# Adding the identity and r to G inside the PSUM bank: two products on TensorE for three additions on VectorE

## The chip, the cores and the metric

The kernel runs on one core of one Trainium2 chip. The metric is the device time of one execution in microseconds (us), the median of the runs of one kernel. The granted TensorE clock is given as a share of full speed: 1.00 is 2.4 GHz and 0.50 is 1.2 GHz.

## The reference, cut to what matters

The whole program is a small two-block network (512 tokens of 1024 channels, two expert layers, a gated MLP, an RWKV layer, two attention layers). The change touches only the recurrence of the RWKV layer:

```python
def _wkv_step(S, inp):
    r_t, w_t, k_t, v_t, a_t, b_t = inp
    sa = jnp.einsum('zbhvk,zbhk->zbhv', S, a_t)
    S = S * w_t[..., None, :] + sa[..., :, None] * b_t[..., None, :] + v_t[..., :, None] * k_t[..., None, :]
    return S, jnp.einsum('zbhvk,zbhk->zbhv', S, r_t)
...
def wkv_bidir(state0, scan_in):
    state, ys = lax.scan(_wkv_step, state0, scan_in)
```

It runs in both directions (z) over 256 context and 512 latent positions, for 16 heads of 64 channels.

## The kernel before, in words

The recurrence is not walked position by position. `rwkv_scan` cuts the 768 positions into 12 chunks of C = 64 (NCH = 12, four of the context and eight latent, `lat`) and the 16 heads into 8 pairs (KD = 8). A head pair is a **group** of 12 chunks; 8 x 12 = 96 chunks, called rounds here, follow one another.

Inside a group the chunks form a chain through the state SV. `Chain.period` issues one round: `py` of chunk g, `pg` of chunk g+1, `pa` of g+3, `ps` and `pz` of g+2 (the table `STAGES`). Each is one PSUM bank with a single buffer (pY, pG, pA, pS, pz), filled by TensorE (PE) and emptied by VectorE (DVE) and ScalarE (ACT):

- `pa` (L1534): the chunk's triangular scores, to SC2 by ACT (L1541) and, masked, by DVE (L1542).
- `ps` (L1544): the transposed k and b and their products with r, to SCB by ACT (L1554) and DVE (L1556).
- `pz` (L1559): SC2 times the solved triangular inverse XF, to Zx by ACT (L1566).
- `pg` (L1568): four products Zx x SCB into the bank pG. The upper 64 partitions of G are copied by ACT (L1583). The lower 64 get the identity added in the first 64 columns (L1575) and, for latent chunks, r times the decay (RH) in the last 64 (L1581, twice), all three on DVE.
- `py` (L1585): four products G x SV into pY. DVE scales the new state into SV (L1596), and the output Y is copied by ACT (L1606) or added by DVE (L1608).

The PE instructions of the chain keep their written order (class `Ordered`). All else is placed by the compiler's scheduler, which writes one fixed order for each engine: an instruction that waits holds up all that stand behind it on its engine.

Beside the chain, the next head pair is prepared: `scan_decay`, `scan_scaled` and `scan_r` compute decays and scaled keys, and `solve` inverts the triangular blocks. `solve` starts with a transposition into Mx on DVE (L1427). Then 62 small multiplications and additions on DVE (L1438 into sol, L1440 into Xx) and 48 on GpSimd (POOL; the same lines, sop) run beside one another; when both are done DVE transposes the result into XR and XL (L1444, L1445). PE takes XR in 24 products pv, ACT copies them to Vs (L1460) after copying parts of XL to XF (L1472), and PE runs 24 products px, which ACT copies to XF. No chunk of the next group can pass `pz` before that.

```python
STAGES = (("py", 0), ("pg", 1), ("pa", 3), ("ps", 2), ("pz", 2))
...
    for e, r0, r1, nm in ((nc.vector, 0, R.rows, "sol"), (nc.gpsimd, R.rows, 31, "sop")):
        for u in range(r0, 31):
```

Of the kernel before, what the change touches and what calls it, by code (L numbers as in the profile page):

```python
# [10 lines left out]
F32 = mybir.dt.float32  # L11
# [5 lines left out]
OP = mybir.AluOpType  # L17
# [3 lines left out]
P = 128  # L21
# [658 lines left out]
def moe(K, l, nt, rows, router, gain=None):  # L680
# [23 lines left out]
    with tc.tile_pool(name="mow", bufs=1) as wb, tc.tile_pool(name="mox", bufs=3) as s2, \  # L704
# [83 lines left out]
        for i, (r, u) in enumerate(units):  # L788
            pu = unit_mm(xT, weights("moe_wu", r), "pu")
            if i + 2 < n:  # L790
                gather(i + 2)
            hg = s2.tile([P, 256], F32, name="hg")
            nc.scalar.activation(hg, pg, AF.Silu)  # L793
            nc.vector.tensor_tensor(out=hg, in0=hg, in1=pu, op=OP.mult)  # L794
            if i + 1 < n:
                pg = unit_mm(xn, weights("moe_wg", units[i + 1][0]), "pg")
            elif gain is not None:
                nc.scalar.dma_start(T.gain, gain)
            hT = unit_hT(hg)
            xT, xn = xn, unit_in(i + 2) if i + 2 < n else None  # L800
            unit_out(i, hT, weights("moe_wd", r))
# [132 lines left out]
def expert_h(K, s2, pg, pu):  # L934
    nc = K.nc
    hg = s2.tile([P, 512], F32, name="hg")
    nc.scalar.activation(hg, pg, AF.Silu)
    nc.vector.tensor_tensor(out=hg, in0=hg, in1=pu, op=OP.mult)
    return hg
# [24 lines left out]
C = 64  # L964
# [215 lines left out]
def two(a, b):  # L1180

    return bass.AP(tensor=a.tensor, offset=a.offset, ap=[list(a.ap[0]), [b.offset - a.offset, 2], *[list(d) for d in a.ap[1:]]])
# [312 lines left out]
class Chain:  # L1495
# [72 lines left out]
    def pg(self, ch):  # L1568
        R, S, lat, nq = self.R, ch.S, ch.lat, ch.nq
        pg = R.p.tile([P, 2, 2, P], F32, name="pG")  # L1570
        for h in range(2):
            for z in range(2):
                self.pe.matmul(pg[:, h, z, :nq], lhsT=ch.Zx[:, h, z, :], rhs=ch.SCB[:, z, :2 if lat else 1, h, :], start=True, stop=True)
        ch.G = G = R.s3.tile([P, 2, 2, P], F32, name="G")
        d = [self.K.nc.vector.tensor_tensor(out=G[:C, :, :, :C].rearrange("p h z t -> p (h z) t"),  # L1575
                               in0=pg[:C, :, :, :C].rearrange("p h z t -> p (h z) t"),
                               in1=R.id2[:C, None, :].to_broadcast([C, 4, C]), op=OP.add)]
        if lat:
            for h in range(2):
                hs = slice(h * C, (h + 1) * C)  # L1580
                d.append(self.K.nc.vector.tensor_tensor(out=G[:C, h, :, C:], in0=pg[:C, h, :, C:],  # L1581
                                       in1=two(S.RH[hs, 0, ch.sl[0], h], S.RH[hs, 1, ch.sl[1], h]), op=OP.add))
        self.apart(self.K.nc.scalar.copy(G[C:, :, :, :nq], pg[C:, :, :, :nq]), d)  # L1583

    def py(self, ch):  # L1585
        R, S, nq, sl, vs, i = self.R, ch.S, ch.nq, ch.sl, ch.vs, ch.i
# [816 lines left out]
```

## Time and profile before

| what | value |
|---|---|
| median of 3 runs | 3281.62 us (3279.72 to 3285.73) |
| the profiled execution: its own time, its span | 3283.3 us, 3281.5 us |
| busy over the span: PE, DVE, ACT, POOL | 89%, 47%, 32%, 23% |
| mean granted TensorE clock | 0.930 |
| the scan's rounds, from the first to the last | about 1457 to 2095 us of the span |

Times of day are in us from the span's start. An engine is busy where one of its instructions runs; a line such as L1575 is a line of the code above. A product of float32 shows as two rows of the trace (two passes), so four products pG are eight passes. Rows of the windows view give the busy time of engines in a stretch, and behind each in brackets the number of instructions.

### The profile page before, as it was taken

The page shows a single profiled execution, that of the slowest core. Times are in us where ns is not written, and L with a number is a line of the kernel's source. Part 1 is how long each engine was busy: PE and PEld are TensorE (multiplying, and loading weights), DVE is VectorE, ACT ScalarE, POOL GpSimd, SP SyncE. Part 2 cuts the span into 40 slices and gives each one's busy share as a digit, 9 for nine tenths or more (in the row PEclk, how much of TensorE's full clock was granted, in tenths as well). Part 3 has the DMA queues.
Part 4 walks back from the last instruction along what each step waited for, and adds up shares of the span by engine and source line. Part 5 has one row for each costly group of instructions (what it writes and reads, how often), then busy time and mean ns, then how long its engine had stood idle before and what let it go on. Part 6 is the DMA issues. An engine that isn't in the chain of part 4 may idle for free. (4 is left out here: it accounts for less than half of the span.)

```text
span 3281.5 us, 51499 instructions
## 1 busy us (share of the span) xinstructions
PE 2909.2 (89%) x18992; PEld 2096.6 (64%) x18992; DVE 1547.4 (47%) x3550; ACT 1036.6 (32%) x2318; POOL 747.4 (23%) x949
## 2 busy tenths in 40 slices
PE   8999997999999799957777777889999987899998
PEld 4777786555554487647777776765555546777866
DVE  4342354100000498678777777541111126665584
ACT  4111231111111343355555555410000014544463
POOL 1022322111111100255556656221111110000000
PEclk9999997999999899968888878889999998999999
DMA  7555516899999624110111110569999994121200
GB/s 287 185 173 188 202 49 251 289 408 408 405 406 404 271 73 146 66 61 24 34 33 38 38 35 18 188 251 399 409 407 405 402 346 144 53 75 61 76 33 33
DMA packets 222836, 637.64 MB, mean 194 GB/s; under 512 B 37779, under 2 KB 65251, under 8 KB 222449
## 3 DMA queue, kind: packets, MB, share of 16 engines
q1 hardware_dynamic: 180048, 565.13, 45.3%
q10 hardware_dynamic: 27472, 45.72, 4.2%
q0 software_dynamic: 15056, 23.41, 2.0%
q8 instruction: 153, 2.51, 0.3%
q14 instruction: 107, 0.87, 0.1%
HBM read 609.24 MB, written 49.00 MB: 201 GB/s over the span
## 5 line engine op out<-in xcount | busy, mean ns | idle before, releaser
L793 ACT ACTIVATE hg<-pg 128x256 f32<-128x256 f32 x86 | 33.0, 383 | 790.4 <-PE pg L1489 790.4
L794 DVE TENSOR_TENSOR hg<-hg,pu 128x256 f32<-128x256 f32 x86 | 36.2, 421 | 522.5 <-PE pu L1489 515.3
L734 POOL DMA_INDIRECT xe<-hrow,idx x86 | 88.2, 1026 | 655.3 <-PE ptr L1489 619.2
L71 DVE TENSOR_TENSOR wl<-wr,wh 128x1024 fp32r<-128x1024 f32 (+1 forms) x140 | 168.9, 1221 | 117.8 <-ACT wh L70 117.1
L158 POOL TENSOR_TENSOR rs_r<-rs_t,nhalf 128x1 f32<-128x1 f32 (+2 forms) x52 | 58.2, 1121 | 728.2 <-DVE rs_t L156 387.6
L141 PE MATMUL ps<-hT,wh 128*128 128x512 f32 (+1 forms) x496 | 188.6, 381 | 6.2 <-DVE q L1951 3.0
L142 PE MATMUL ps<-hT,wh 128*128 128x512 f32 (+1 forms) x496 | 183.8, 371 | 0.0
L143 PE MATMUL ps<-hT,wl 128*128 128x512 f32 (+1 forms) x496 | 183.3, 370 | 0.0
L70 ACT CAST wh<-wr 128x1024 fp32r<-128x1024 f32 (+1 forms) x140 | 141.2, 1041 | 126.9 <-PE ps L143 45.4
L1489 PE MATMUL pu<-wx,xT 128*64 128x256 f32 x1520 | 176.8, 380 | 4.8 <-DMA wx<-in_moe_wu 4.8
L1489 PE MATMUL pd<-wx,hT 128*64 128x512 f32 x704 | 161.9, 598 | 18.4 <-issue 10.0
L1489 PE MATMUL pg<-wx,xT 128*64 128x256 f32 x1520 | 174.2, 379 | 1.1 <-DMA wx<-in_moe_wg 0.8
L764 DVE COPY hT<-pth 128x128 f32<-128x128 f32 x86 | 25.1, 292 | 313.6 <-ACT hT L763 313.6
L1489 PE MATMUL pd<-we,hT 128*64 128x512 f32 x672 | 155.1, 599 | 11.8 <-issue 6.5
L1489 PEld LDWEIGHTS pu<-wx,xT 128*64 128x64 f32 x1520 | 110.4, 137 | 84.3 <-issue 24.7
L1489 PE MATMUL pG<-SCB,Zx 128*128 128x128 f32 (+1 forms) x768 | 118.6, 303 | 39.3 <-DVE SCB L1556 19.0
L1489 PE MATMUL pu<-we,xT 128*64 128x256 f32 x1232 | 143.4, 380 | 6.8 <-DMA we<-in_moe_wu 6.7
L1489 PE MATMUL pg<-we,xT 128*64 128x256 f32 x1232 | 145.9, 387 | 2.8 <-DMA we<-in_moe_wg 1.2
L1489 PEld LDWEIGHTS pg<-wx,xT 128*64 128x64 f32 x1520 | 111.8, 137 | 54.7 <-issue 2.1
L779 POOL DMA_INDIRECT ybuf<-yo,idx x86 | 86.4, 1005 | 234.4 <-ACT yo L776 84.5
L1489 PEld LDWEIGHTS pG<-SCB,Zx 128*128 128x128 f32 x768 | 104.0, 210 | 47.8 <-ACT Zx L1566 29.0
L1489 PEld LDWEIGHTS pu<-we,xT 128*64 128x64 f32 x1232 | 88.6, 137 | 67.7 <-issue 15.6
(583 smaller groups left out, 6881.4 us busy)
## 6 DMA issues: line engine op xcount, KB each, us to landing
wx<-in_moe_wu SPq DMA_DIRECT2D x144, 512.0 KB
wx<-in_moe_wg SPq DMA_DIRECT2D x144, 512.0 KB
wx<-in_moe_wd SPq DMA_DIRECT2D x130, 512.0 KB
we<-in_moe_wd SPq DMA_DIRECT2D x126, 512.0 KB
we<-in_moe_wg SPq DMA_DIRECT2D x112, 512.0 KB
we<-in_moe_wu SPq DMA_DIRECT2D x112, 512.0 KB
w<-in_ada_w SPq DMA_DIRECT2D x96, 512.0 KB
wr<-in_ga_w_in SPq DMA_DIRECT2D x32, 512.0 KB
```

Source lines behind the costliest of these rows:

```text
L70: nc.scalar.copy(hi, x)
L71: nc.vector.tensor_tensor(out=lo, in0=x, in1=hi.bitcast(F32), op=OP.subtract)
L141: nc.tensor.matmul(ps, lhsT=a[0], rhs=b[0], start=start, stop=False, **kw)
L142: nc.tensor.matmul(ps, lhsT=a[0], rhs=b[1], start=False, stop=False, **kw)
L143: nc.tensor.matmul(ps, lhsT=a[1], rhs=b[0], start=False, stop=stop, **kw)
L158: nc.gpsimd.tensor_tensor(out=r, in0=t, in1=K.nhalf[:, :n], op=OP.pow)
L734: nc.gpsimd.indirect_dma_start(out=xe[i % 3], out_offset=None, in_=hhalf, in_offset=bass.IndirectOffsetOnAxis(ap=idx[:, u, 0, r:r + 1], ax ...
L764: nc.vector.tensor_copy(hT[:, 1], pt[:, 1])
L779: nc.gpsimd.indirect_dma_start(out=yhalf, out_offset=bass.IndirectOffsetOnAxis(ap=idx[:, u, 1, r:r + 1], axis=0), in_=yo, in_offset=None, ...
L793: nc.scalar.activation(hg, pg, AF.Silu)
L794: nc.vector.tensor_tensor(out=hg, in0=hg, in1=pu, op=OP.mult)
L1489: r = f(*a, **kw)
```

## The change

The four products of pG now open one accumulation over the whole bank. Two more products follow: id2 (two stacked 64 x 64 identities) times the identity matrix adds the identity to the first 64 columns of the lower half, in every round; id2 times RH adds r to the last 64 columns, in rounds of latent chunks. One ACT copy then takes all 128 partitions of G. The three additions on DVE are gone.

```diff
     def pg(self, ch):
         R, S, lat, nq = self.R, ch.S, ch.lat, ch.nq
         pg = R.p.tile([P, 2, 2, P], F32, name="pG")
+        f = dict(skip_group_check=True)
         for h in range(2):
             for z in range(2):
-                self.pe.matmul(pg[:, h, z, :nq], lhsT=ch.Zx[:, h, z, :], rhs=ch.SCB[:, z, :2 if lat else 1, h, :], start=True, stop=True)
-        ch.G = G = R.s3.tile([P, 2, 2, P], F32, name="G")
-        d = [self.K.nc.vector.tensor_tensor(out=G[:C, :, :, :C].rearrange("p h z t -> p (h z) t"),
-                               in0=pg[:C, :, :, :C].rearrange("p h z t -> p (h z) t"),
-                               in1=R.id2[:C, None, :].to_broadcast([C, 4, C]), op=OP.add)]
+                self.pe.matmul(pg[:, h, z, :nq], lhsT=ch.Zx[:, h, z, :], rhs=ch.SCB[:, z, :2 if lat else 1, h, :],
+                               start=(h == 0 and z == 0), stop=False, **f)
+
+        self.pe.matmul(pg[:C, :, :, :C], lhsT=R.id2, rhs=self.K.ident.rearrange("p (h t) -> p h t", h=2)[:, :, None, :].to_broadcast([P, 2, 2, C]),
+                       start=False, stop=True, **f)
         if lat:
-            for h in range(2):
-                hs = slice(h * C, (h + 1) * C)
-                d.append(self.K.nc.vector.tensor_tensor(out=G[:C, h, :, C:], in0=pg[:C, h, :, C:],
-                                       in1=two(S.RH[hs, 0, ch.sl[0], h], S.RH[hs, 1, ch.sl[1], h]), op=OP.add))
-        self.apart(self.K.nc.scalar.copy(G[C:, :, :, :nq], pg[C:, :, :, :nq]), d)
+            self.pe.matmul(pg[:C, :, :, C:].rearrange("p h z t -> p z h t"), lhsT=R.id2, rhs=two(S.RH[:, 0, ch.sl[0]], S.RH[:, 1, ch.sl[1]]),
+                           start=False, stop=True, **f)
+        ch.G = R.s3.tile([P, 2, 2, P], F32, name="G")
+        self.K.nc.scalar.copy(ch.G[:, :, :, :nq], pg[:, :, :, :nq])
```

The scheduler also writes another order. On PE, at the end of a solve in the middle of the scan, before (pY, pG, pA, pS are the chain's, pv and px the solve's):

```order
L1489 MATMUL pY<-SV,G 128x64 x4
L1489 MATMUL pG<-SCB,Zx_10725 128x128 x4
L1489 MATMUL pA<-BK_10717,AD_10719 128x128 x2
L1489 MATMUL pS<-ident,BK_10717 128x128 x2
L1458 MATMUL pv<-XR,MO 64x64 x24
L1458 MATMUL px<-XL,Vs 64x64 x24
```

And with the change:

```order
L1489 MATMUL pY<-SV,G 128x64 x4
L1458 MATMUL pv<-XR,MO 64x64 x24
L1489 MATMUL pG<-SCB,Zx_10725 128x128 x4
L1489 MATMUL pG<-ident,id_9924 64x4x64
L1489 MATMUL pG<-RI_10455,id_9924 64x2x2x64
L1489 MATMUL pA<-BK_10717,AD_10719 128x128 x2
L1489 MATMUL pS<-ident,BK_10717 128x128 x2
L1458 MATMUL px<-XL,Vs 64x64 x24
```

The products pv have moved ahead of the round's pG, pA and pS, and these now stand between pv and px.

On DVE, before, one round within the solve (SV to SV; sol and Xx are steps of the solve):

```order
L1596 TENSOR_TENSOR SV<-pY,WL 64x2x128
L1608 TENSOR_TENSOR Y<-pY,Y 64x128 x2
L1438 TENSOR_TENSOR sol<-Xx,Mx 128x98
L1575 TENSOR_TENSOR G<-pG,id_9924 64x4x64
L1581 TENSOR_TENSOR G<-pG,RI_10455 64x2x64 x2
L1440 TENSOR_TENSOR Xx<-Xx,sol 128x7x14
L1542 TENSOR_TENSOR SC_13360<-pA,mL 128x2x64
L1438 TENSOR_TENSOR sol<-Xx,Mx 128x91
L1440 TENSOR_TENSOR Xx<-Xx,sol 128x7x13
L1556 TENSOR_TENSOR SCB<-pS,mR 128x2x128
L1438 TENSOR_TENSOR sol<-Xx,Mx 128x84
L1440 TENSOR_TENSOR Xx<-Xx,sol 128x7x12
```

With the change, the end of the same solve:

```order
L1542 TENSOR_TENSOR SC_13292<-pA,mL 128x2x64
L1438 TENSOR_TENSOR sol<-Xx,Mx 128x21
L1440 TENSOR_TENSOR Xx<-Xx,sol 128x7x3
L1556 TENSOR_TENSOR SCB<-pS,mR 128x2x128
L1438 TENSOR_TENSOR sol<-Xx,Mx 128x14
L1440 TENSOR_TENSOR Xx<-Xx,sol 128x7x2
L1596 TENSOR_TENSOR SV<-pY,WL 64x2x128
L1438 TENSOR_TENSOR sol<-Xx,Mx 128x7
L1608 TENSOR_TENSOR Y<-pY,Y 64x128 x2
L1440 TENSOR_TENSOR Xx<-Xx,sol 128x7
L1444 STREAM_TRANSPOSE XR<-Xx 128x1024
L1445 STREAM_TRANSPOSE XL<-Xx 128x1024
```

Before, the rounds of the chain ran out at the step of 84 elements and 24 steps in a row followed; with the change the steps are spread over the rounds down to the last, and between Mx and XR stand no G, and two SC, one SCB, one SV and two Y (one row of x2) fewer.

## Rows read from the trace of the kernel before

**Rows 1.** Windows of all engines: the scan's rounds (busy PE, PEld, DVE, ACT, POOL; clock).

```profile
core 0: us, PE busy (x) PEld busy (x) DVE busy (x) ACT busy (x) POOL busy (x), PEclk, DMA share, GB/s
1457.50:2095.40 637.90, 493.44 (x4248) 459.31 (x4248) 498.25 (x1162) 344.40 (x877) 365.46 (x485) 0.82 0.11 33
```

**Rows 2.** Waits in the scan: who waited for whom, us in total, times, longest.

```profile
POOL Xx L1430 <- DVE XL L1445: 61.6, 6, 12.2
PE pv L1458 <- DVE XR L1444: 53.6, 7, 8.2
...
PE px L1458 <- ACT Vs L1460: 14.3, 7, 2.1
```

**Rows 3.** Windows of the seven solves, Mx to XR, all engines: their sum.

```profile
sum 258.00, PE 182.98 PEld 172.65 DVE 244.68 ACT 118.63 POOL 169.87; mean PE 26.14 PEld 24.66 DVE 34.95 ACT 16.95 POOL 24.27
```

**Rows 4.** The same seven windows, tile sol alone (DVE's solve): shortest, longest, sum.

```profile
1741.20:1776.90 35.70, 20.08 (x62) 0.98 0.08 23
...
1996.90:2035.90 39.00, 23.45 (x62) 0.98 0.08 21
sum 258.00, DVE 148.53; mean DVE 21.22
```

**Rows 5.** The same seven windows, tile G alone: their sum.

```profile
sum 258.00, PE 52.08 PEld 48.24 DVE 44.98 ACT 29.04; mean PE 7.44 PEld 6.89 DVE 6.43 ACT 4.15
```

**Rows 6.** The same seven windows, tile sop alone (POOL's part of the solve): their sum.

```profile
sum 258.00, POOL 151.46; mean POOL 21.64
```

**Rows 7.** Timeline at the end of one solve (start, us, instruction).

```profile
1684.51 0.25 POOL L1440 TENSOR_TENSOR Xx<-Xx,sop 128x24 f32<-128x24 f32 x1
...
1691.43 1.25 DVE L1444 STREAM_TRANSPOSE XR<-Xx 128x1024 f32<-128x1024 f32 x1
1692.60 1.86 DVE L1445 STREAM_TRANSPOSE XL<-Xx 128x1024 f32<-128x1024 f32 x1
...
1692.73 4.45 PE L1458 MATMUL pv<-XR,MO 32*64 32x64 f32 x48 [7.45 <-DVE XR L1444]
1694.49 3.41 ACT L1472 COPY XF<-XL 32x384 f32<-32x384 f32 x4 [8.65 <-DVE XL L1445]
...
1697.91 2.58 ACT L1460 COPY Vs<-pv 32x192 f32<-32x192 f32 x8
...
1699.23 4.44 PE L1458 MATMUL px<-XL,Vs 32*64 32x64 f32 x48 [2.06 <-ACT Vs L1460]
```

**Rows 8.** Groups by line in the scan: the G instructions, and a copy of 128 partitions.

```profile
L1575 DVE TENSOR_TENSOR G<-pG,id 64x256 f32<-64x256 f32 x95 | 39.1, 411 | 9.9 <-PE pG L1489 8.9
L1583 ACT COPY G<-pG 64x512 f32<-64x512 f32 x64 | 37.2, 581 | 88.7 <-issue 65.7 <-PE pG L1489 13.7 <-ACT Y L1606 4.2
L1581 DVE TENSOR_TENSOR G<-pG,RI 64x128 f32<-64x128 f32 x128 | 35.5, 278 | 1.9
L1554 ACT COPY SCB<-pS 128x256 f32<-128x256 f32 x95 | 35.4, 373 | 19.9 <-PE pS L1489 17.2 <-DVE km L1406 2.3 <-PE pz L1489 0.3
...
L1583 ACT COPY G<-pG 64x256 f32<-64x256 f32 x31 | 11.4, 367 | 31.0 <-PE pG L1489 18.1 <-DVE SC L1542 4.0 <-DMA kT<-kD 3.3
```

**Rows 9.** Groups of the page, expert layers: products with 64 columns of weights, 256 moving.

```profile
L1489 PE MATMUL pu<-wx,xT 128*64 128x256 f32 x1520 | 176.8, 380 | 4.8 <-DMA wx<-in_moe_wu 4.8
```

**Rows 10.** Windows of two pA (four passes each): busy PE, clock.

```profile
1717.60:1718.90 1.30, 1.17 (x4) 0.50 0.00 0
1723.00:1723.70 0.70, 0.66 (x4) 1.00 0.70 225
```

**Rows 11.** Windows, all engines: four rounds of the last group; then 17 us behind a solve.

```profile
2071.10:2084.40 13.30, 13.30 (x122) 13.30 (x121) 8.12 (x24) 9.87 (x29) 0.00 (x0) 1.00 0.13 41
1690.00:1707.00 17.00, 12.21 (x110) 11.60 (x111) 7.37 (x14) 9.44 (x22) 1.53 (x2) 0.50 0.00 1
```

**Rows 12.** Windows of the six stretches px to the next Mx: all engines, then tile G.

```profile
sum 220.50, PE 183.87 PEld 165.80 DVE 166.22 ACT 135.83 POOL 157.76; mean PE 30.65 PEld 27.63 DVE 27.70 ACT 22.64 POOL 26.29
...
sum 220.50, PE 28.75 PEld 25.98 DVE 15.18 ACT 12.30; mean PE 4.79 PEld 4.33 DVE 2.53 ACT 2.05
```

**Rows 13.** Timeline of a solve: a DVE step beside a long POOL instruction.

```profile
1829.76 1.04 POOL L1640 TENSOR_TENSOR vt<-vt,bon 128x512 f32<-128x512 f32 x1 [0.57 <-DMA vt<-vD]
1829.87 1.17 DVE L1438 TENSOR_TENSOR sol<-Xx,Mx 128x135 f32<-128x135 f32 x1
```

## The prediction

> **What bounds the kernel now.** The change touches nothing outside the scan, so I read the windows view of the scan first [rows 1]: of 637.9 us DVE is busy 498.3 (78%), PE 493.4 (77%), POOL 365.5, ACT 344.4. That is an average over stretches with different limits, so the next view is the list of waits [rows 2]. Its long entries belong to the solve: PE's products pv wait 53.6 us in seven waits (7.7 each) for DVE's XR, and POOL waits 10.3 us on average for XL before it may clear Xx for the next group.
>
> The third view is the windows of the seven solves that run beside the chain, each from Mx to XR. In 258.0 us (36.9 each) DVE is busy 244.7, that is 95%, PE only 183.0 [rows 3]. So DVE paces that stretch, and XR, which ends it, is the event that PE waits for. DVE's work in it: 62 steps of the solve, 21.2 us on average [rows 4], and the G additions, 45.0 us in all or 6.4 per solve [rows 5]. The remaining DVE work is the chain's SC, SCB, SV and Y.
>
> The timeline at the end of one solve shows what follows [rows 7]: XR 1691.43, pv when it is done, ACT's copies XF and Vs, px until 1703.67, so 12.2 us from XR to the end of px, all one after another. From px to the next Mx pass 36.8 us on average, in which PE is busy 30.7 and DVE 27.7 [rows 12]: no engine is alone the limit there. In the last group there is no preparation left: four rounds take 13.30 us and PE is busy for all of it [rows 11].
>
> **What the change removes.** One addition of the identity per round at 0.41 us and 128 of r at 0.28 leave DVE, about 75 us of busy time [rows 8]. What counts is where they stood.
>
> *In the solves.* Without G, DVE has 6.4 us less to do between Mx and XR. The new order also sets two SC, one SCB, one SV and two Y behind XR. I price them by the G rows of the same width [rows 8], 128 elements at 0.28 and 256 at 0.41: 4 x 0.28 + 2 x 0.41 = 1.94 us. Together 8.4. Two things hold that back. XR needs POOL's half too: POOL resumed 10.3 us behind its last step [rows 2], of which XR and XL take 3.0 [rows 7], so its half leads by 7.2 us and that is the cap. And the denser steps of DVE meet POOL's instructions more often. What such meetings cost shows between solves: 62 steps take 20.1 us in the shortest and 23.5 in the longest [rows 4], 3.4 more, and 8.4 less 3.4 is 5.0, the lower end. I take **6.0 per solve**, in the middle of 5.0 and 7.2: 7 x 6.0 = **42 us gained** (35 to 50).
>
> One meeting stands in the timeline: a step of 135 elements took 1.17 us because a POOL instruction of 512 elements, begun 0.11 us before, ran until 1830.80 [rows 13]. The Trainium skill goes further (SBUF — State Buffer, section SBUF: two separate sides): a VectorE instruction with two SBUF inputs and a GpSimd one that reads SBUF take turns on a port pair, and the second waits for the whole of the first. By that rule G, with one input in PSUM, is just the kind that can run beside POOL, and the solve would have no room to shrink. The trace agrees for the long instruction of rows 13 and disagrees for the short steps as a whole: sol 21.2 and sop 21.6 us [rows 4, 6] make 42.9, more than the 36.9 in which both are done.
>
> **What it adds.** *Products on PE.* The nearest row with 64 columns of weights and 256 moving ones took 176.8 us for 1520 passes, 0.116 each [rows 9], so 0.23 us for a product of two passes: 0.23 per context round, 0.47 per latent one. At clock 0.50 four passes took 1.17 against 0.66 at 1.00 [rows 10], a factor of 1.8, so up to 0.82 per latent round. Below: nothing, where PE is waiting anyway. In the solves PE has 26.1 of 36.9 us busy [rows 3], six rounds add 2.8, and DVE still paces: that cover is DVE's own load, and if it were gone a round would cost what it does in the last group. There nothing covers: 8 x 0.47 + 4 x 0.23 = 4.7, **5 us lost**.
>
> *Between px and Mx.* Four context rounds and one latent add 1.4 us to PE at full clock, 2.5 at the low one; DVE loses 2.5 of G [rows 12]. So -2.5 to +2.5; PE is the busier of the two, and I take +0.7 for each of seven (six stretches, and the one ahead of the first solve, taken alike): **5 us lost**.
>
> *ACT's copy.* It takes all 128 partitions. 256 elements took 0.367 us from 64 partitions and 0.373 from 128 [rows 8], so the copy of 512 stays at 0.58: nothing added. G is complete 0.47 us later, but the two r additions and the identity (0.97 on DVE) no longer follow, and between pG and the pY that reads it PE runs pA, pS and pz. Queued behind the copy on ACT are SC, SCB and Zx; they shift by 0.47 at most, and PE by no more than the products already counted.
>
> *Behind XR.* pv now comes before the round's pG, the two products, pA and pS, which then stand ahead of px. Fourteen passes at 0.165 [rows 10] and 0.47 are 2.8 us. At the full clock pv and px shrink by 1.8 to 2.5 each: 1.3 + 2.5 + 2.8 = 6.6 behind XR's start, while Vs is there only at 7.8 as before (ACT copies XF first [rows 7]); px would end at 10.3, 1.9 earlier. At the low clock it is 1.3 + 4.45 + 4.9 + 4.44 = 15.1, 2.9 later. Before, PE had waited 7.45 us ahead of pv and the granted clock was 0.50 for the 17 us around it [rows 7, 11]; in the new order DVE reaches XR right after the round's SV, and PE has a round of its own to do first, so it should hardly wait. I take -1.0, nearer to the full clock: **7 us gained**.
>
> **The sum.** -42 - 7 + 5 + 5 = -39 us on the profiled execution's 3283.3 (span 3281.5): 3244.3. That execution is 1.7 us above the median of 3281.62, which gives **3243**. With all best ends, 50 + 13 + 18 - 5 = 76 us gained, it is 3206; with all worst, 35 - 20 - 18 - 5 = 8 us lost, 3290.
>
> **Rivals.**
>
> *The solve doesn't end earlier (slower).* If DVE and POOL steps hold one another up so that Mx to XR stays near 36.9 us, the 42 us fall away, PE waits before pv as now, the clock is low there, and the moved round costs 2.9 each: 7 x 2.9 + 5 + 5 = 30 us, **3312**. It decides where the solve gains less than 30 / 7 = 4.3 us. For it: POOL is busy 24.3 of 36.9 us there [rows 3], and rows 13. Against it: sum of rows 4 and 6 as above. Chance 0.14. The port rule of the Trainium skill, cited above, would end here.
>
> *Half the gain.* The steps gain 3.0 us per solve, the clock behind XR brings nothing: -21 + 10 = -11, **3271**. Chance 0.13.
>
> *More.* The cap of 7.2 is reached, pv and px run at the full clock, and the stretch after px profits from it (1.2 each): -50 - 13 - 8 + 5 = -66, **3216**. For it: PE falls to 0.50 only where it has waited [rows 7, 11]. Against it: the cap is another engine's end, and all three must come together. Chance 0.15.
>
> *That it doesn't do what it says* is ruled out for the removal (the order shows no G on DVE); that the scheduler's order undoes it is the first rival.
>
> **How the numbers follow.** My forecast, 3225 to 3262, has 0.58. 0.2% (6.6 us, to 3275) is about what a measurement of this kernel can tell from no change. Faster: 0.58 + 0.15 and 0.05 of the half gain, 0.78; same 0.08, the rest of the half gain; slower 0.14. The range leaves out the slower rival and a little of each end: 3212 to 3276.
>
> **What would show it.** Right: windows Mx to XR of about 31 us with DVE still above 90%; PE's wait for XR far below 53.6 us; rounds of the last group at 3.8 instead of 3.33; all instructions of G gone from DVE and the new products at 0.23 us. Wrong: sol well above 21.2 us or XR released by POOL (first rival); pv still behind a wait and at clock 0.50 (no second gain); px to Mx over 38 us; a product of over 0.3 us at the full clock.

## The result, and the profile after

The changed kernel takes 3304.32 us (median of four runs, 3297.04 to 3308.21), the kernel before beside it 3281.86. The ratio is 1.0059 with a 95% interval of 1.0044 to 1.0074: 0.6% slower, where 3243 us had been forecast. The profiled execution is the fastest of the four (3297.04 us, span 3294.9). Set against the profile before, the scan ends 18 us later, and the rest of that execution was 5 us shorter, which no run explains.

By the stretches of the prediction (each taken from the windows views; for before, [rows 3, 12] and the seven windows from XR to the end of px):

| stretch | before | forecast, in all | after | measured, in all |
| --- | --- | --- | --- | --- |
| Mx to XR, seven solves | 36.9 us each | -42 | 33.8 each | -21.6 |
| XR to the end of px, seven | 12.2 each | -7 | 16.8 each | +32 |
| px to the next Mx (six measured, seven forecast) | 36.8 each | +5 | 36.2 each | -3 |
| last group, from px to its end | 47.3 | +5 | 57.3 | +10 |

Windows of all engines after the change: the scan, which answers to [rows 1].

```profile
1457.50:2113.60 656.10, 586.33 (x4571) 493.96 (x4570) 464.81 (x941) 343.05 (x879) 360.33 (x485) 0.87 0.11 32
```

VectorE's 498 us fell to 465, as meant; PE went from 493 to 586, and with 89% busy it is now the busiest engine of the scan. The solves (the sum of seven windows), then the same windows for tile sol and for tile sop alone, answering to [rows 3, 4, 6]:

```profile
sum 236.40, PE 205.50 PEld 172.97 DVE 219.45 ACT 101.92 POOL 161.13; mean PE 29.36 PEld 24.71 DVE 31.35 ACT 14.56 POOL 23.02
...
sum 236.40, DVE 173.60; mean DVE 24.80
...
sum 236.40, POOL 148.76; mean POOL 21.25
```

A solve is 3.1 us shorter instead of 6.0. VectorE's own 62 steps grew from 21.2 to 24.8 us. The windows from XR to the end of px, one of the seven and the sum; then the six windows from px to the next Mx; then four latent rounds of the last group, answering to [rows 11, 12]:

```profile
1691.10:1708.30 17.20, 17.20 (x141) 14.72 (x139) 6.84 (x12) 10.27 (x24) 1.12 (x2) 0.78 0.02 5
...
sum 117.90, PE 117.83 PEld 101.74 DVE 47.75 ACT 71.51 POOL 6.70; mean PE 16.83 PEld 14.53 DVE 6.82 ACT 10.22 POOL 0.96
...
sum 217.10, PE 182.74 PEld 152.33 DVE 160.66 ACT 128.46 POOL 163.64; mean PE 30.46 PEld 25.39 DVE 26.78 ACT 21.41 POOL 27.27
...
2081.40:2099.60 18.20, 18.20 (x139) 15.55 (x138) 4.53 (x12) 10.01 (x29) 0.00 (x0) 1.00 0.06 15
```

Behind XR PE is busy all the time, and still the stretch is 4.6 us longer. A round of the last group takes 4.55 us, 1.2 more than before, at the same full clock. The groups by line show what the new instructions cost on average over the scan, both clock levels mixed (the ACT copy is the last one):

```profile
L1489 PE MATMUL pG<-ident,id 128*64 128x256 f32 x190 | 69.5, 451 | 0.0
...
L1489 PE MATMUL pG<-RI,id 128*64 128x256 f32 x128 | 42.3, 415 | 0.0
...
L1583 ACT COPY G<-pG 128x512 f32<-128x512 f32 x64 | 37.5, 587 | 144.5 <-PE pG L1489 142.6 <-PE pz L1489 1.9
```

A pass occupies PE for 0.37 and 0.33 us (69.5 / 190 and 42.3 / 128), three times the 0.116 of [rows 9]; the copy keeps its 0.58. The waits of the scan: PE's wait for XR (53.6 us in [rows 2]) is gone from the list, and others wait for PE.

```profile
ACT G L1583 <- PE pG L1489: 153.5, 70, 6.1
...
POOL Xx L1430 <- DVE XL L1445: 41.1, 6, 8.7
...
PE pG L1489 <- DVE SCB L1556: 26.1, 25, 2.1
```

Where the two large differences sit is seen in two timelines. First PE in one latent round of the last group, at the full clock (start, us, instruction):

```profile
2086.76 1.11 PE L1489 MATMUL pG<-SCB,Zx 128*128 128x128 f32 x8
2087.80 0.65 PE L1489 MATMUL pG<-ident,id 128*64 128x256 f32 x2
2088.29 0.59 PE L1489 MATMUL pG<-RI,id 128*64 128x256 f32 x2
2088.81 0.71 PE L1489 MATMUL pA<-BK,AD 128*128 128x128 f32 x4
2089.36 0.27 PE L1489 MATMUL pS<-ident,BK 128*128 128x128 f32 x1
```

The same place before:

```profile
2071.91 1.11 PE L1489 MATMUL pG<-SCB,Zx 128*128 128x128 f32 x8
2072.86 0.61 PE L1489 MATMUL pA<-BK,AD 128*128 128x128 f32 x4
2073.30 0.27 PE L1489 MATMUL pS<-ident,BK 128*128 128x128 f32 x1
```

From start to start, pG takes 1.04 us, the identity 0.49, r 0.52, pA 0.55. Before, pG took 0.95 and pA 0.44. So 1.01 us are the products and 0.20 more lie on their neighbours. Between two passes of one product the distance is 0.215 us for 256 columns. Four of them make 0.86, and the other 0.34 to 0.35 of the 1.21 appear where the weights change from 128 columns to 64 and back.

The second is PE at the end of one solve (XR begins at 1691.09), and below it the windows of its four pieces:

```profile
1691.78 0.71 PE L1489 MATMUL pA<-BK,AD 128*128 128x128 f32 x4
...
1693.44 1.00 PE L1489 MATMUL pY<-SV,G 128*128 128x64 f32 x8
...
1694.37 4.25 PE L1458 MATMUL pv<-XR,MO 32*64 32x64 f32 x48
...
1698.55 2.08 PE L1489 MATMUL pG<-SCB,Zx 128*128 128x128 f32 x8
1700.56 1.12 PE L1489 MATMUL pG<-ident,id 128*64 128x256 f32 x2
1701.47 1.06 PE L1489 MATMUL pG<-RI,id 128*64 128x256 f32 x2
1702.46 1.22 PE L1489 MATMUL pA<-BK,AD 128*128 128x128 f32 x4
...
1704.04 4.30 PE L1458 MATMUL px<-XL,Vs 32*64 32x64 f32 x48
```

```profile
1691.10:1694.37 3.27, 3.27 (x26) 2.74 (x24) 3.24 (x3) 1.88 (x5) 0.04 (x1) 1.00 0.09 26
1694.37:1698.55 4.18, 4.18 (x49) 4.06 (x48) 3.31 (x9) 4.08 (x8) 1.07 (x2) 0.86 0.00 0
1698.55:1704.04 5.49, 5.49 (x19) 3.78 (x18) 0.00 (x0) 2.69 (x8) 0.00 (x0) 0.50 0.00 0
1704.04:1708.27 4.23, 4.23 (x50) 4.11 (x49) 0.29 (x1) 1.61 (x6) 0.00 (x0) 0.90 0.01 2
```

XR is no longer waited for: PE is still at the round before and begins pv 3.3 us behind XR's start (1.3 before). Then the granted clock falls, to 0.50 behind pv, though PE had no pause, and the round that the new order put between pv and px runs at that clock: 5.49 us.

### The profile page after: what moved, and what is told of

Same layout as the page of the kernel before. It is cut to its first block, busy times and chain, and to the rows that moved or that the text cites. A ratio compares the mean times of both kernels' runs of the same rounds, so it can differ in the third digit from the quotient of the medians.

```text
span 3294.9 us, 51894 instructions
## 1 busy us (share of the span) xinstructions
PE 3000.9 (91%) x19312; PEld 2133.8 (65%) x19312; DVE 1513.8 (46%) x3326; ACT 1035.8 (31%) x2318; POOL 740.2 (22%) x949
## 5 line engine op out<-in xcount | busy, mean ns | idle before, releaser
L794 DVE TENSOR_TENSOR hg<-hg,pu 128x256 f32<-128x256 f32 x86 | 36.2, 421 | 518.0 <-PE pu L1489 518.0
L158 POOL TENSOR_TENSOR rs_r<-rs_t,nhalf 128x1 f32<-128x1 f32 (+2 forms) x52 | 45.5, 877 | 714.3 <-DVE rs_t L156 653.1
L1489 PEld LDWEIGHTS pG<-SCB,Zx 128*128 128x128 f32 x768 | 106.4, 214 | 53.2 <-ACT Zx L1566 21.2
```

The source lines that it names most:

```text
L158: nc.gpsimd.tensor_tensor(out=r, in0=t, in1=K.nhalf[:, :n], op=OP.pow)
L1489: r = f(*a, **kw)
```

## The experiments

The theory after this reading: the price taken from [rows 9] is half of what a pass costs, changes of weight width come on top, and so PE paces where VectorE did. The rivals were the gaps in the output and the repeated moving operand, the new order on PE, and a solve that cannot end much earlier. All medians stand beside the kernel before on the same chip; "round" is a regular latent round of the last group. The expectations use means over six rounds, the last of which is shorter (3.27, 4.13, 4.47 where the regular round is 3.34, 4.21, 4.55). "Mx to Mx" is the sum of three means: seven solves, seven stretches from XR to the end of px, six from there to the next Mx.

| kernel | ratio to before (95%) | round | Mx to XR | XR to px's end | Mx to Mx |
| --- | --- | --- | --- | --- | --- |
| before | 1 | 3.34 | 36.9 | 12.2 | 85.9 |
| the change | 1.0059 (1.0044 to 1.0074) | 4.55 | 33.8 | 16.8 | 86.8 |
| no products | 0.9925 (0.9912 to 0.9939) | 3.34 | 33.4 | 11.9 | 81.5 |
| products on top of before | 1.0043 (1.0030 to 1.0057) | 4.55 | 38.4 | 11.0 | 85.9 |
| weights of 128 columns | 0.9992 (0.9983 to 1.0001) | 4.21 | 33.0 | 14.7 | 83.4 |
| identity in bfloat16 | 0.9970 (0.9960 to 0.9980) | 4.20 | 34.2 | 11.2 | 81.7 |
| both | 0.9946 (0.9933 to 0.9958) | 3.89 | 34.4 | 11.2 | 81.7 |
| r to the other half of the array | 0.9937 (0.9918 to 0.9956) | 4.12 | 33.7 | 11.7 | 82.1 |
| order of before | 1.0008 (0.9999 to 1.0017) | 4.55 | 33.0 | 15.4 | 84.8 |
| 128 columns and order of before | 0.9998 (0.9988 to 1.0008) | 4.21 | 32.9 | 15.1 | 83.9 |
| identity in bfloat16, r on VectorE | 0.9988 (0.9976 to 1.0001) | 3.92 | 36.5 | 11.7 | 84.4 |
| mixed | 0.9928 (0.9915 to 0.9940) | 3.34 | 34.5 | 11.2 | 82.3 |
| mixed, 6 rows | 0.9959 (0.9945 to 0.9973) | 3.34 | 35.6 | 11.2 | 82.8 |

### The relief alone, and the products alone

The products are left out:

```diff
-        self.pe.matmul(pg[:C, :, :, :C], lhsT=R.id2, rhs=self.K.ident.rearrange("p (h t) -> p h t", h=2)[:, :, None, :].to_broadcast([P, 2, 2, C]),
-                       start=False, stop=True, **f)
-        if lat:
-            self.pe.matmul(pg[:C, :, :, C:].rearrange("p h z t -> p z h t"), lhsT=R.id2, rhs=two(S.RH[:, 0, ch.sl[0]], S.RH[:, 1, ch.sl[1]]),
-                           start=False, stop=True, **f)
```

> Leaves out the identity and r altogether (G is the bare product, one copy of ScalarE), so only the relief of VectorE is left. T expects latent rounds of the last group at 3.33 us as before the change, XR to the end of px about 12 us, Mx to XR 31 to 33 us instead of 36.9, and 3240 to 3262 us in all: the gain that the prediction had, without the products' price. Rival (S): the solve can't end earlier than about 34 us, since GpSimd's half or collisions on the way hold it up even with a free PE: Mx to XR 33.5 to 35, in all 3262 to 3275.

3259.1 us against 3282.6. The time is in T's interval (at most 3262), but the solve, 33.4 us, is longer than T's 31 to 33 and stands next to the rival's 33.5 (sums of the seven windows, all engines and tile sol).

```profile
sum 233.80, PE 179.92 PEld 173.41 DVE 217.73 ACT 114.40 POOL 162.14; mean PE 25.70 PEld 24.77 DVE 31.10 ACT 16.34 POOL 23.16
...
sum 233.80, DVE 161.78; mean DVE 23.11
```

So even with free products the relief is worth 3.5 us per solve and some 24 us in all, not 42. The forecast's first term was nearly twice too large before any product is counted. And the solve is nearly the same with the products (33.8) and without (33.4), with VectorE busy 93% of either: there it is still VectorE that paces, not PE.

The products with zero weights on the kernel before, VectorE's additions kept:

```diff
...
+        nc.vector.memset(R.id2z, 0.0)
...
+        self.pe.matmul(pg[:C, :, :, :C], lhsT=R.id2z, rhs=self.K.ident.rearrange("p (h t) -> p h t", h=2)[:, :, None, :].to_broadcast([P, 2, 2, C]),
+                       start=False, stop=True, **f)
+        if lat:
+            self.pe.matmul(pg[:C, :, :, C:].rearrange("p h z t -> p z h t"), lhsT=R.id2z, rhs=two(S.RH[:, 0, ch.sl[0]], S.RH[:, 1, ch.sl[1]]),
+                           start=False, stop=True, **f)
```

> The kernel before with the two products added on top, their weights zero, and the three additions of VectorE kept: the products' price alone. T expects latent rounds of the last group at 4.5 us (+1.2), so 8 x 1.2 + 4 x 0.6 = 12 us there, and in the solves and between them part of 1.2 us per round as well, since VectorE waits for G's bank later: 3300 to 3330 us in all. Rival (C): outside the last group the products are covered by the waits of PE, and only those 12 us show: 3290 to 3296.

3298.2 against 3282.6, between the two. The last group pays 10 us as T said, but from Mx to Mx it takes 85.9 us as before (38.4 + 11.0 + 36.5): while VectorE paces, the products are covered, as the rival said. The same products that cost 5.3 us per group once VectorE is relieved (86.8 against 81.5) cost none there. Of the 5.3 the solve has 0.4; 4.9 lie behind XR, 16.8 us against 11.9.

### What makes a product long

```diff
...
+        nc.vector.memset(R.id2w[:, C:], 0.0)
+        nc.vector.tensor_copy(R.id2w[:, :C], R.id2)
...
-        self.pe.matmul(pg[:C, :, :, :C], lhsT=R.id2, rhs=self.K.ident.rearrange("p (h t) -> p h t", h=2)[:, :, None, :].to_broadcast([P, 2, 2, C]),
+        self.pe.matmul(pg[:, :, :, :C], lhsT=R.id2w, rhs=self.K.ident.rearrange("p (h t) -> p h t", h=2)[:, :, None, :].to_broadcast([P, 2, 2, C]),
...
-            self.pe.matmul(pg[:C, :, :, C:].rearrange("p h z t -> p z h t"), lhsT=R.id2, rhs=two(S.RH[:, 0, ch.sl[0]], S.RH[:, 1, ch.sl[1]]),
+            self.pe.matmul(pg[:, :, :, C:].rearrange("p h z t -> p z h t"), lhsT=R.id2w, rhs=two(S.RH[:, 0, ch.sl[0]], S.RH[:, 1, ch.sl[1]]),
```

> Theory (T): a 256-column float32 pass costs what its columns cost, 0.215 us at the full clock, also where two passes of the expert layer's row ran side by side in two halves of the array; the rest of the 1.20 us by which a latent round of the last group grew (some 0.34) is the change between weights of 128 and of 64 columns. Here both products take weights of 128 columns (the right half zeros) and write all 128 partitions, nothing else moves. T expects passes still 0.215 apart, the step into them and out of them as between any two passes, latent rounds of the last group at about 4.2 us instead of 4.55, and 3285 to 3295 us in all (after: 3304). Rival (P): a pass is slow because its output has gaps or because its moving operand repeats the identity; both stay, so rounds stay at 4.5 us and the time within 4 us of 3304.

3279.4 against 3282.6: 25 us less than the change, more than T expected. PE begins pv 1.6 us behind XR's start instead of 3.2, and from XR to the end of px it is 14.7 us instead of 16.8. PE in a round, as above:

```profile
2061.14 1.11 PE L1492 MATMUL pG<-SCB,Zx 128*128 128x128 f32 x8
2062.09 0.60 PE L1492 MATMUL pG<-ident,id2w 128*128 128x256 f32 x2
2062.52 0.59 PE L1492 MATMUL pG<-RI,id2w 128*128 128x256 f32 x2
2062.95 0.61 PE L1492 MATMUL pA<-BK,AD 128*128 128x128 f32 x4
2063.40 0.27 PE L1492 MATMUL pS<-ident,BK 128*128 128x128 f32 x1
```

Now 0.95, 0.43, 0.43 and 0.45 us: each product costs two passes of 0.215, and pG and pA are back at their old length. The change of width cost 0.34 us per latent round, whatever the pattern of output and operands (P falls). The Trainium skill (TensorEngine Tiling (Array Packing), section Key Properties) says that changing the tiling mode drains TensorE; the trace agrees in that time is lost at each change, 0.34 us for a way there and back.

Identity alone in bfloat16, with 64 columns of weights as in the change:

```diff
...
+        nc.vector.tensor_copy(R.id2b, R.id2)
+        nc.vector.tensor_copy(R.idb, K.ident)
...
-        self.pe.matmul(pg[:C, :, :, :C], lhsT=R.id2, rhs=self.K.ident.rearrange("p (h t) -> p h t", h=2)[:, :, None, :].to_broadcast([P, 2, 2, C]),
+        self.pe.matmul(pg[:C, :, :, :C], lhsT=R.id2b, rhs=R.idb.rearrange("p (h t) -> p h t", h=2)[:, :, None, :].to_broadcast([P, 2, 2, C]),
```

> The identity product alone is made of bfloat16 operands (0 and 1 are exact in it), with the same output and the same moving pattern; the product of r stays float32. T expects one pass instead of two, about 0.11 us long plus the change of weights, so latent rounds of the last group near 4.2 us, context rounds 0.4 shorter than after. The order has pv behind the round's pS again, as before the change, so XR to the end of px should come back from 16.9 us towards 13 to 14. In all 3265 to 3285 us. Rival P (the output's gaps decide): the one pass costs 0.25 or more, rounds 4.3 or more. Rival O (the place of pv in PE's order, not the products' length, made XR to px longer): XR to px back at 12 to 13 us although a round still has three passes more than before.

3271.9 against 3282.6, within T's interval; rounds 4.20, and XR to px better than either expected. This kernel has nearly the round of the one with wide weights (4.20 and 4.21) but not its order: pv stands behind the round's pG, pA and pS, and on VectorE XR comes one round later. The two are 1.7 us apart from Mx to Mx (81.7 and 83.4), and the orders on PE and VectorE are the likely cause; the section on the order varies PE's alone.

Both remedies:

```diff
-        self.pe.matmul(pg[:, :, :, :C], lhsT=R.id2w, rhs=self.K.ident.rearrange("p (h t) -> p h t", h=2)[:, :, None, :].to_broadcast([P, 2, 2, C]),
+        self.pe.matmul(pg[:, :, :, :C], lhsT=R.id2b, rhs=R.idb.rearrange("p (h t) -> p h t", h=2)[:, :, None, :].to_broadcast([P, 2, 2, C]),
```

(against the kernel with wide weights; `id2b` too has 128 columns here)

> Both remedies together: the identity from bfloat16 operands and both products with weights of 128 columns. T expects a latent round of the last group at 3.27 + one pass of 0.11 + two of 0.215 = 3.8 us, against 4.13 and 4.12 with one remedy each; from Mx to Mx 81.5 us, where the kernel without any product stands (so the covered part is free); in all 3262 to 3270. Rival: the change from float32 to bfloat16 weights costs as much as the change of width did; then the round stays at 4.0 or more and the time at 3270 to 3276.

3269.7 against 3285.6. The regular round is 3.89 = 3.34 + 0.11 + 0.43 (3.81 as a mean over six), and Mx to Mx 81.7, next to the 81.5 without products: T.

Why [rows 9] showed half:

```diff
-            self.pe.matmul(pg[:C, :, :, C:].rearrange("p h z t -> p z h t"), lhsT=R.id2, rhs=two(S.RH[:, 0, ch.sl[0]], S.RH[:, 1, ch.sl[1]]),
-                           start=False, stop=True, **f)
+            self.pe.matmul(pg[C:, :, :, C:].rearrange("p h z t -> p z h t"), lhsT=R.id2, rhs=two(S.RH[:, 0, ch.sl[0]], S.RH[:, 1, ch.sl[1]]),
+                           start=False, stop=True, tile_position=(0, C), **f)
```

> Measures why the row that the price was taken from showed half. Leaves the lower half of G without r: the product of r, still float32 with weights of 64 columns, goes to the other 64 columns of the array and so to the upper half of the bank, where it doesn't belong; the identity product is as in the change. Theory H (in the expert layer two products in the two halves of the array run at the same time, so a row divided by its passes shows half of what one costs): passes of the two products now begin in pairs, and a latent round of the last group takes 3.27 + 2 x 0.215 + 0.34 = 4.04 us instead of 4.47. Rival (a pass with 256 columns is cheap in the expert layer for its operands): passes stay one behind the other, 4.47. The order has pv behind pS, so in all 3270 to 3282 under H, near 3288 (as with that order alone) under the rival.

3267.5 against 3284.3, below what H expected; a round is 4.04 us as a mean over six, as H has it. The timeline of PE in a round:

```profile
2057.22 1.11 PE L1489 MATMUL pG<-SCB,Zx 128*128 128x128 f32 x8
2058.26 0.43 PE L1489 MATMUL pG<-ident,id 128*64 128x256 f32 x1
2058.26 0.43 PE L1489 MATMUL pG<-RI,id 128*64 128x256 f32 x1
2058.53 0.38 PE L1489 MATMUL pG<-ident,id 128*64 128x256 f32 x1
2058.53 0.38 PE L1489 MATMUL pG<-RI,id 128*64 128x256 f32 x1
2058.84 0.71 PE L1489 MATMUL pA<-BK,AD 128*128 128x128 f32 x4
```

The passes begin in pairs; the two products together take 0.58 us instead of 1.01. H holds: the expert layer writes its products with 64 columns of weights to the two halves of the array in turn, two run at once, and busy time divided by passes gives half of one. The trace of the kernel before shows it without any run: the passes of the row in [rows 9] begin two by two, mostly 7 ns apart, and the next two some 0.21 us later. A stretch of the same form there (pg):

```profile
605.18 3.62 PE L1489 MATMUL pg<-we,xT 128*64 128x256 f32 x32
```

One behind the other at 0.215 us, 32 passes would take 7.0 us; 16 pairs take the 3.62. "Different tiles can execute LdWeights and Matmul in parallel" says the Trainium skill (TensorEngine Tiling (Array Packing), section Key Properties), and the pairs agree.

### The order on PE

One edge for the scheduler: pv behind the round's last pS.

```diff
...
+        if ch.i == 0 and ch.g:
+            for m in S.px:
+                self.K.tc.add_manual_dep(m, last.ins.name, mybir.DependencyInfo(mybir.DependencyClass.NoSync, mybir.DependencyReason.DATA), reason="order")
```

> The changed kernel with its two float32 products of 64-column weights as they are, and one thing put back: the solve's products pv stand behind the round's pG, pA and pS again, as before the change. Theory O (the order that the change brought with it costs by itself): XR to the end of px falls from 16.9 us to 11 to 12 (with the products on top of the kernel before it was 11.0 in this order), and since the round then stands ahead of XR, Mx to XR may grow by 1 to 3 us; from one Mx to the next 83 to 85 us instead of 86.8, in all 3283 to 3296. Rival W (only the amount of PE's work counts, whatever its order): what XR to px gains comes back ahead of XR or behind px, 86 to 87 us from Mx to Mx, in all 3300 to 3308.

3288.6 against 3285.6; 84.8 us from Mx to Mx, in O's interval, but not by O's mechanism: XR to px's end is 15.4, because XR is still early on VectorE and pv starts 7.1 us behind it. What was gained is that the round's products stand ahead of pv, at the higher clock: in the solve that ends at 1687.3 us the round ahead of pv takes 3.0 us at 1.00, where the change has 5.49 at 0.50 behind it.

The same edge in the kernel with weights of 128 columns:

> Weights of 128 columns in both float32 products, and pv behind pS as before the change: the fourth corner beside the change (neither), the wide weights alone and the order alone. If the two add up, the wide weights' 25 us and the order's 16 give 3263 to 3268; if both take away the same lateness of PE behind XR (the rival, which I take for likelier), the second one brings only part, 3270 to 3277, with Mx to Mx at 81.7 to 82.5 us against 83.4 and 84.8 with one alone.

3283.8 against 3284.3, slower than either outcome expected: with wide weights the same edge brings nothing (0.9998 against 0.9992). So the order costs up to 0.5% with the narrow weights, and no value of its own can be given to it; what the kernels with the better order have beside it, a place for XR that fits it on VectorE, wasn't tried alone.

### One part of the change, and a mixture

Identity in bfloat16 with wide weights, r on VectorE, ScalarE copying the rest:

```diff
...
+            for h in range(2):
+                hs = slice(h * C, (h + 1) * C)
+                d.append(self.K.nc.vector.tensor_tensor(out=G[:C, h, :, C:], in0=pg[:C, h, :, C:],
+                                       in1=two(S.RH[hs, 0, ch.sl[0], h], S.RH[hs, 1, ch.sl[1], h]), op=OP.add))
+            self.K.nc.scalar.copy(G[:C, :, :, :C], pg[:C, :, :, :C])
+            self.apart(self.K.nc.scalar.copy(G[C:], pg[C:]), d)
...
```

> One part of the change alone, at its cheapest: the identity by one bfloat16 product of 128-column weights, r added by VectorE as before the change, and ScalarE copies the rest of G in two pieces. T expects last-group rounds of 3.4 us, Mx to XR between the 36.9 of before and the 33.4 without any addition (VectorE keeps 3.9 us of r per solve), some 35.5, and Mx to Mx 84; in all 3268 to 3276. Rival (the products matter less than VectorE's load): slower than with r on PE by more than 8 us, 3276 or more. Rival (r is what PE cannot afford): faster than with r on PE, below 3262.

3283.7 against 3285.6: in the first rival's interval. Mx to XR is 36.5 us, 1 more than T expected; and two copies of G (0.37 and 0.58) lengthen ScalarE's part, so that PE waits for G in the last group (round 3.92).

In the last group as before the change, elsewhere both remedies:

```diff
+        if ch.g // NCH == KD - 1:
...
+            return
```

> As the kernel with both remedies, but in the last group, where PE alone is the limit and no solve runs on VectorE, G is made as before the change, with three additions on VectorE and no product. T expects the last group at 47 us as before (its own 44.9 without any addition) instead of about 50, nothing else changed, so 2 to 4 us less than with both remedies everywhere: 3259 to 3267. Rival: the additions' waits there cost as much as the products did, no difference.

3261.2 against 3285.6, in T's interval: the fastest kernel that still adds both, 0.7% faster than before. The last group takes 45.2 us instead of 49.6. Its windows from XR to px (one, and the sum) show the better order: no round between pv and px.

```profile
1686.10:1697.10 11.00, 9.81 (x104) 9.25 (x102) 5.72 (x7) 8.11 (x19) 1.21 (x2) 0.78 0.01 2
...
sum 78.60, PE 70.22 PEld 66.19 DVE 39.94 ACT 57.35 POOL 7.38; mean PE 10.03 PEld 9.46 DVE 5.71 ACT 8.19 POOL 1.05
```

With `ROWS = 6` instead of 7:

> The mixed kernel with one more row of the solve moved from VectorE to GpSimd (6 and 25 instead of 7 and 24). If VectorE still paces the solve and GpSimd has its lead of some 5 us to give (in the mixed kernel it ends that much earlier), Mx to XR falls by 1 to 2 us and the time by 7 to 14, to 3247 to 3254. Rival: the longer GpSimd half meets more of VectorE's steps and ends last, no gain or a loss, 3261 or more.

3273.0 against 3284.3, by the ratios 10 us more than the mixed kernel: the rival's time, but not its way. GpSimd does not end last, it still ends 5.0 us before XR (5.6 in the mixed kernel). VectorE's steps, which were to shrink, take 24.9 us instead of 24.1, and its last step now stands 2.3 us before XR instead of 0.5, with instructions of the chain between. So the lead could not be spent; why the steps grew was not tried.

### Where the rest of a solve's gain went

```diff
+        if nm == "sop" and c:
+            nc.gpsimd.memset(tmp[:, :1], 0.0)
```

> The changed kernel, but GpSimd may begin its half of a solve only when VectorE has done the last step of its own (GpSimd first clears one element that this step reads), so the two no longer run side by side; slower by design. If VectorE's 62 steps took 24.8 us per solve instead of 21.2 because they meet GpSimd's instructions more often, they take 17 to 18.5 us here, about what the sum of the shortest times of each step is (17.3), and Mx to the last step about 26 us. Rival: the steps are slower for another reason (waits for the chain, writes into the same tile), 21 us or more.

Inconclusive: 3307.2 against 3286.3 (one run of each), and the trace has GpSimd clearing the element at the end of its half, both halves still side by side (sol 24.5 us). The next one ties the data itself:

```diff
+        if nm == "sop" and c:
+            nc.gpsimd.tensor_scalar(X[:, r0:r0 + 1, r0:r0 + 1], X[:, 0:1, 31:32], 0.0, 1.0, op0=OP.mult, op1=OP.add)
```

> The changed kernel with GpSimd's half of each solve truly behind VectorE's: its first step reads an element of the diagonal that it rewrites as 1.0 from one that VectorE's last step writes (in the earlier try GpSimd only cleared an element at its own end, and both halves still ran side by side). Slower by design, by some 15 to 20 us per solve. If VectorE's 62 steps took 24.8 us per solve instead of 21.2 because they meet GpSimd's instructions more often, they take 17 to 18.5 us here, near the sum of the shortest times of each step in the kernel before (17.3). Rival: the steps are slower for another reason (waits for the chain, writes into the same tile), 21 us or more.

3397.8 against 3288.9 (one run of each). The seven solves, tile sol and tile sop alone:

```profile
sum 367.60, DVE 127.74; mean DVE 18.25
...
sum 367.60, POOL 141.32; mean POOL 20.19
```

The first outcome: alone, VectorE's 62 steps take 18.2 us; beside GpSimd they took 21.2 before, 23.1 without products and 24.8 in the change. So of the 6.4 us of G, 3.6 came back as longer steps (24.8 less 21.2).

## Why the prediction was wrong

**The price of a product** is the step that failed: "0.116 each, so 0.23 us for a product of two passes", with a lower bound of nothing and an upper one of 0.82 per round. Busy time over passes was read as the cost of one pass, where two ran at once. Measured: 0.215 per pass, and 0.34 per round for the change of weight width, 1.21 per latent round instead of 0.47; a product of over 0.3 us had been named as what would make the forecast wrong. The row of the scan's own pG was nearer in every respect but shape: passes of 128 columns there begin every 0.112 us, which for 256 makes 0.22. With products of 0.54 per latent round, near the forecast's 0.47, the kernel is 0.5% faster than before instead of 0.6% slower. That one has another order too, and how much of the difference is the order's stays open. Two more terms failed beside the price, the solves and the stretch behind XR.

**The solves (-42, measured -21.6).** The direction was right, all of G left VectorE and it stays at 93% (219.45 of 236.4). The size was not. G's 6.4 us and the 1.9 of moved instructions did leave. More meetings with GpSimd had been given 3.4 us, but as the lower end, and 6.0 was put above it; the steps grew by 3.6. Also, neighbouring rows of VectorE overlap (after the change SCB began at 1689.15 for 0.42 us and the next step at 1689.48), so removed durations, added up, are more than the busy time they free: that fell by 3.6 us per solve (34.95 to 31.35), where 6.4 + 1.9 - 3.6 says 4.7. VectorE's idle time grew by 0.5, which leaves the 3.1. Of the Trainium skill's rule (SBUF — State Buffer, section SBUF: two separate sides) the runs bear out half: VectorE's steps pay for GpSimd beside them, up to 6.6 of 24.8 us. They don't bear out turns throughout: the two halves take 18.2 + 20.2 = 38.4 us when apart, and both are done in 33.8.

**Behind XR (-7, measured +32).** This is the largest miss. "PE should hardly wait" came true. "Nearer to the full clock" did not: the clock fell from pv on with PE busy throughout, so it falls without a wait too. And the full clock would not have brought the gain, for "at the full clock pv and px shrink by 1.8 to 2.5 each" is wrong. In the mixed kernel one pv runs at 1.00 from start to end:

```profile
1687.40 4.14 PE L1466 MATMUL pv<-XR,MO 32*64 32x64 f32 x47 [0.47 <-DVE XR L1452]
...
1687.30:1691.60 4.30, 4.20 (x51) 4.21 (x52) 4.21 (x7) 2.45 (x7) 1.21 (x2) 1.00 0.02 6
```

That is 4.2 us, against 4.45 at 0.50 before [rows 7, 11]. The factor had been taken from pA, with other shapes. With 4.2 the forecast's working for the full clock gives 1.3 + 4.2 + 2.8 + 4.2 = 12.5 us to px's end, no gain on 12.2. The working for the low clock gave 15.1; PE's own lateness, 3.2 instead of 1.3, makes it 17.0, and 16.8 was measured. That it fits is in part luck: in the solve shown the two products took 1.90 us between pv and px (1700.56 to 1702.46) where the working had 0.82, and pv, px, pG, pA and pS about 1.0 less than it had. The fourteen passes were priced too high because the 0.66 of [rows 10] for four holds the end of the last one; in a row they begin every 0.112 us, not 0.165.

**The last group (+5, measured +10)** failed by the price: from the first latent pG to the end it grew by 9.1 us, where eight times 1.21 says 9.7. The four context rounds grew by 1.0 in all, where four products at 0.43 each would be 1.7 without any change of width; so "there nothing covers" did not hold for them. **Px to Mx (+5, measured -3)** lies within its bounds. **ACT's copy** stayed at 0.587 as said.

**The cover.** That the products are free only as long as VectorE paces was stated, and the runs show it: on top of the kernel before they cost nothing from Mx to Mx. In the relieved solve VectorE still paces, and they are covered there too (33.8 us with them, 33.4 without), although PE is busy for 29.4 of the 33.8. What was overlooked is the stretch that follows: PE comes late to pv, and a round with its products stands between pv and px. With both remedies from Mx to Mx it is 81.7 us, next to 81.5 without products, so relief and cover can be had together where products are short and the order is another.

The slower rival (3312) came nearest in time, in part by luck. Its threshold held, a gain of 3.1 us is under 4.3, and its cause, longer steps beside GpSimd, is half of the story. But its terms were no gain in the solves and 20 us lost behind XR, where 22 were gained and 32 lost; the wait before pv that it expected did not return.

## What to carry to other kernels

A price taken from a group of rows needs a look at whether its instructions ran one after another: busy time divided by count is a cost only then. Before work is moved from the engine that paces to another, the other engine's load should be added up with the moved work, in that stretch and in the one behind it: here the solve covered the products, and the stretch behind XR paid. A factor between two clocks holds for the shape that it was measured on. And operands that keep an engine in the mode it is in (here weights padded with zeros to 128 columns, or bfloat16 for a matrix of 0 and 1) can cost less than the smaller, seemingly cheaper form.

## What the runs showed of the hardware

- A float32 pass with 64 columns of weights is no shorter than one with 128: 0.215 us for 256 moving columns in both, at the full clock. One bfloat16 pass of them took 0.11.
- Going from weights of 128 columns to 64 and back cost 0.34 us around two products.
- The granted clock fell from 1.00 to 0.50 (1.2 GHz) over the 48 passes of pv (32 rows, 64 columns) although PE was busy without a gap; it stayed there for the round behind them, and px, of the same kind, ran at 0.90 on average.
- Those passes of pv hardly depend on the clock: 48 took 4.2 us at 1.00 (mixed kernel) and 4.45 at 0.50 (before). The eight passes of pG took 1.11 and 2.08 at the two levels.
- In the changed kernel VectorE's small steps beside GpSimd's took a third longer than alone (24.8 against 18.2), GpSimd's only 5% longer (21.25 against 20.19).
